# Seven products of a Strassen-like step, all in one matmul form, in 22 of 32 pairs

## The chip, the cores and the metric

The kernel runs on one core of one Trainium2 chip. The metric is the device time of one execution in microseconds (us); of three runs the median is 1759.95 us (1758.12 to 1761.29). Engines: PE (TensorE) multiplies matrices into PSUM, eight banks of 512 float32 columns on 128 partitions; DVE (VectorE) and ACT (ScalarE) do elementwise work and read PSUM; POOL (GpSimd) and SP (SyncE) here mostly issue DMAs. Each engine works its own instructions off in order and waits for semaphores.

## The reference

Two layers on 512 tokens of width 1024. Each layer has a feed-forward half step, a mixer (convolution, window attention and memory attention side by side) and a second feed-forward half step:

```python
def swiglu(x, w1, w3, w2):
    return (jax.nn.silu(x @ w1) * (x @ w3)) @ w2
...
        h = x + 0.5 * swiglu(rms_norm(x, ffn1_norm[l]), ffn1_w1[l], ffn1_w3[l], ffn1_w2[l])
        ...
        h = h + 0.5 * swiglu(rms_norm(h, ffn2_norm[l]), ffn2_w1[l], ffn2_w3[l], ffn2_w2[l])
```

`w1` and `w3` are 1024 x 2816 and `w2` is 2816 x 1024, all float32. So there are four feed-forwards, here called the parts, and they hold most of the matmul work.

## The kernel before

**Precision.** A float32 operand is split into two parts of a shorter format (`hi` by an ACT copy that rounds, `lo` by a DVE subtraction of `hi` from the operand). A product of two operands is three matmul passes: hi x hi, hi x lo, lo x hi. `split` (L147 to L149) does this, and `unit` (L357) does it for one weight tile of 128 x 1024 into a pair of tiles `whi` and `wlo`, of which there are four pairs in turn.

**The up projection.** The 2816 columns of `w1` and `w3` are 22 blocks of 128. The first four blocks of a part are computed plainly. The others go in pairs of blocks (f, f+1), nine in a part, through `up_pair` (L362). There each of the two matrices is multiplied by a two-by-two block scheme with seven products instead of eight: the weights of a pair and the activations (1024 rows in two halves, 512 tokens in two halves of 256) are added and subtracted in a fixed pattern, and seven products of 512 rows x 128 columns x 256 tokens are combined by additions. `Seven` (L297) prepares the seven moving operands `m[1]` to `m[7]`, each as four row blocks k, and each block with its hi part and its lo part of 256 columns beside each other. The weights' sums are made by DMAs that accumulate (the tile `wsum`, called X: block f by SP, then block f+1 added by POOL, L369 and L370) and, for the raw sums, by two DVE adds (L400) in the raw tile itself. A pair has seven weight units: raw and raw (one for each matrix; products 1 and 2), raw sum and raw sum (products 6 and 3), X and X (products 7 and 5), and z for both matrices (product 4).

**Two forms of a product.** `product` (L377) makes twelve matmuls of 256 columns that accumulate in one place: for each k, whi with the hi part and whi with the lo part, then four times wlo with the hi part. `beside` (L384) makes eight: four of 512 columns, in which whi meets the hi and the lo part at once and the two results stand beside each other in one PSUM bank, and four of 256 columns, wlo with the hi part, onto the first half. Whoever reads such a bank has to add its two halves, which takes one DVE add more. Before the change, products 1, 6 and 5 of each matrix are in the first form and 2, 3, 7 and 4 in the second; the first pair of each part (f = 4, `PLAIN`) has all of them in the first form, in a branch of its own. So 32 pairs are in the mixed form.

**Sums in PSUM.** Products 1, 6 and 5 of matrix i accumulate onto each other in the tile `x[i]` (tag "pt", two banks). After product 1 ACT copies it to `part[i]` (L438); after product 6 it copies the sum of both (L449), and after product 5 the sum of all three (L458). Products 2, 3, 7 and 4 have banks "po", "cf" and "mm", and `summed` (L402) adds both halves of such a bank and a part. Then come the SiLU (L467), the gate multiplication (L468), and the split of the gated result (L471, L472) for the down projection.

**Order.** The 22 blocks are worked off in quarters of 6, 6, 6 and 4 (`QUARTERS`). In each but the last, the up projection runs one pair ahead; then follows the down projection of the quarter, eight output blocks d with one weight unit each (L149 again, 768 columns) and one addition to the residual `h` (L564). So the pairs come in runs: f = 4 and 6 in the first quarter, 8, 10 and 12 in the second, 14, 16 and 18 in the third, 20 in the last. In the first feed-forward of a layer, the mixer's tables and memory keys (`prepare`) are computed after the first quarter's down projection, beside the second run of pairs.

The order on each engine is not the program's order: a scheduler that simulates the engines' time fills each engine's queue with what it expects to be ready. `tc.issue_after(x)` tells it that what follows is not to be issued ahead of x. Tiles come from pools with a fixed number of buffers, and a new tile waits until the old one in its buffer has been read: three for `raw` (raw, raw and z of a pair), three for X (tag "aux"), four for whi and wlo, one for `u`, two for `g`, two for `part`.

Of the kernel before, what the change touches and what calls it, by code (L numbers as in the profile page):

```python
# [13 lines left out]
AF = mybir.ActivationFunctionType  # L14
# [4 lines left out]
P = 128  # L19
# [8 lines left out]
QUARTERS = ((0, 6), (6, 6), (12, 6), (18, 4))  # L28
# [37 lines left out]
def trunk(ctx: ExitStack, tc: tile.TileContext, xT, memT, pos, w1a, w3a, w2a, w1b, w3b, w2b,  # L66
# [45 lines left out]
    first = []  # L112
# [243 lines left out]

    def unit(x):  # L357
        p = pair()
        split(p[0], p[1], x, V)
        return p  # L360

    def up_pair(l, w13, f, M):  # L362

        raw = [raw_tile(w13[i][l, f], D) for i in range(2)]
        X = []
        for i in range(2):

            x = wst.tile([P, UNIT], F32, tag="aux", name="wsum", bufs=3)
            nc.sync.dma_start(x.rearrange("p (f c) -> p f c", f=2), w13[i][l, f : f + 2, :, 0:QW].rearrange("f p c -> p f c"))  # L369
            G.dma_start(x, w13[i][l, f + 1], accum_op=ALU.add)  # L370
            X.append(x)
        z = wst.tile([P, UNIT], F32, tag="raw", name="raw", bufs=3)
        for i in range(2):
            nc.sync.dma_start(z[:, blk(i, QW)], w13[i][l, f + 1, :, QW:])
        x0, x1 = blk(0, QT), blk(1, QT)

        def product(ps, w, half, j, first=False):  # L377


            for n, (part, q) in enumerate([(0, q) for k in range(4) for q in ((k, 0), (k, 1))] + [(1, (k, 0)) for k in range(4)]):  # L380
                tail[0] = T.matmul(ps, w[part][:, blk(4 * half + q[0])], M.m[j][q[0]][:, q[1]], skip_group_check=True,  # L381
                                   start=first and not n, stop=n == 11)

        def beside(ps, w, half, j, first=False):  # L384


            def go(out, part, n):
                for k in range(4):
                    tail[0] = T.matmul(out, w[part][:, blk(4 * half + k)], M.m[j][k][:, 0:n], skip_group_check=True,  # L389
                                       start=first and not part and k == 0, stop=part == 1 and k == 3)  # L390

            go(ps, 0, 2)
            go(ps[:, 0], 1, 1)

        u, g = (tmp.tile([P, 2, S], F32, tag=t, name=t, bufs=n) for t, n in (("u", 1), ("g", 2)))
        part = [tm("part", "sq", 2) for _ in range(2)]
        to = (u, g)

        def add(out, a, b):
            V.tensor_tensor(out=out, in0=a, in1=b, op=ALU.add)  # L400

        def summed(out, ps, a):  # L402
            add(out, ps[:, 0], a)
            add(out, out, ps[:, 1])

        if f == PLAIN:
            xy = [bank([P, S], "po") for _ in range(2)]
            zv = [bank([P, S], "pt") for _ in range(2)]
            for i in range(2):
                w = unit(raw[i])  # L410
                product(xy[i][:, x0], w, 0, 1, first=True)
                product(xy[i][:, x1], w, 1, 2)
                A.activation(part[i], xy[i], AF.Copy)
                add(to[i][:, 0, x0], part[i][:, x0], part[i][:, x1])

                add(raw[i][:, 0:QW], raw[i][:, 0:QW], X[i][:, QW:])
                add(raw[i][:, QW:], raw[i][:, QW:], raw[i][:, 0:QW])
            for i in range(2):
                w = unit(raw[i])
                product(xy[i][:, x0], w, 0, 6)  # L420
                A.activation(part[i][:, x1], xy[i][:, x0], AF.Copy)
                product(zv[i][:, x0], w, 1, 3, first=True)
            for i in range(2):
                w = unit(X[i])
                product(xy[i][:, x0], w, 1, 5)
                A.activation(part[i][:, x0], xy[i][:, x0], AF.Copy)
                product(zv[i][:, x1], w, 0, 7)
                add(to[i][:, :, x1], zv[i].rearrange("p (n t) -> p n t", n=2), part[i][:, x0].unsqueeze(1).to_broadcast([P, 2, QT]))
            w = unit(z)
            for i in range(2):  # L430
                product(zv[i][:, x1], w, i, 4)
                add(to[i][:, 1, x0], zv[i][:, x1], part[i][:, x1])
        else:
            x = [bank([P, QT], "pt") for _ in range(2)]
            for i in range(2):
                w = unit(raw[i])
                product(x[i], w, 0, 1, first=True)
                A.activation(part[i][:, x0], x[i], AF.Copy)  # L438
                y = bank([P, 2, QT], "po")
                beside(y, w, 1, 2, first=True)  # L440
                summed(to[i][:, 0, x0], y, part[i][:, x0])

                add(raw[i][:, 0:QW], raw[i][:, 0:QW], X[i][:, QW:])
                add(raw[i][:, QW:], raw[i][:, QW:], raw[i][:, 0:QW])
            c, v = [bank([P, 2, QT], t) for t in ("cf", "mm")], []
            for i in range(2):
                w = unit(raw[i])
                product(x[i], w, 0, 6)
                A.activation(part[i][:, x1], x[i], AF.Copy)  # L449
                beside(c[i], w, 1, 3, first=True)  # L450
            for i in range(2):
                w = unit(X[i])
                v.append(bank([P, 2, QT], "po"))
                beside(v[i], w, 0, 7, first=True)
                A.activation(to[i][:, 1, x1], v[i][:, 0], AF.Copy)
                add(to[i][:, 1, x1], to[i][:, 1, x1], v[i][:, 1])
                product(x[i], w, 1, 5)
                A.activation(part[i][:, x0], x[i], AF.Copy)  # L458
                summed(to[i][:, 0, x1], c[i], part[i][:, x0])
                add(to[i][:, 1, x1], to[i][:, 1, x1], part[i][:, x0])  # L460
            w = unit(z)
            for i in range(2):
                beside(v[i], w, i, 4)
                summed(to[i][:, 1, x0], v[i], part[i][:, x1])
        out = gated()
        for n, sign in enumerate((1.0, -1.0)):
            A.activation(u[:, n], u[:, n], AF.Silu, scale=sign)  # L467
        M.gated = V.tensor_tensor(out=g, in0=g, in1=u, op=ALU.mult)  # L468
        for n, sign in enumerate((1.0, -1.0)):
            hi, lo = out[n]  # L470
            A.activation(hi, g[:, n], AF.Copy, scale=sign)  # L471
            V.scalar_tensor_tensor(out=lo, in0=g[:, n], scalar=sign, in1=hi.bitcast(F32), op0=ALU.mult, op1=ALU.subtract)  # L472
        return out

    def ffn(l, w13, w2, x, sums, factors, last, at_product, aside=None, closing=None):
# [60 lines left out]
        for q, (f0, nf) in enumerate(QUARTERS):  # L536
            ahead = 2 if q + 1 < len(QUARTERS) else 0
            for f in range(f0, f0 + nf + ahead, 2):
                if f not in g:
                    g[f], g[f + 1] = up_pair(l, w13, f, M)  # L540
                    if f == PLAIN:
                        with tc.issue_after(M.gated.ins):
                            rescale = after()
            begun = []

            def begin(d):

                w = weights(w2[l, d, :, f0 * P : (f0 + nf) * P], nf * P, V)
                ps = bank([P, S], "mm")
                for j in range(nf - 2):  # L550
                    mm3(ps, at(w, ALL, blk(j)), g[f0 + j], j == 0, False)
                begun.append((ps, w))

            for d in range(KD if ahead or not closing else KD - 2):
                while len(begun) < (d + 1 if ahead or d else 3):
                    with nullcontext() if ahead or d else queued():
                        begin(len(begun))
                ps, w = begun[d]
                for j in range(nf - 2, nf):
                    mm3(ps, at(w, ALL, blk(j)), g[f0 + j], False, j == nf - 1)  # L560
                if not q and rescale:
                    with tc.issue_after((added if d else M.gated).ins):
                        rescale(d)
                added = V.scalar_tensor_tensor(out=h[:, d, :], in0=ps, scalar=0.5, in1=h[:, d, :], op0=ALU.mult, op1=ALU.add)  # L564
                if not ahead:
                    last(d)
            if closing and not ahead:
                closing(l, f0, nf, g, [at(p, ALL, slice(0, nf * P)) for p in
                                       (weights(w2[l, d, :, f0 * P : (f0 + nf) * P], nf * P, V) for d in range(KD - 2, KD))])
            if aside and not q:  # L570
                aside(added)
# [751 lines left out]
```

## Time and profile before

| What | Value |
|---|---|
| median of three runs | 1759.95 us (1758.12 to 1761.29) |
| profiled execution, its own time | 1760.35 us |
| its span, first to last instruction | 1758.5 us |
| instructions | 26405, of them 10004 matmuls |
| busy share PE, PEld, DVE, ACT, POOL | 99%, 87%, 78%, 52%, 11% |
| granted PE clock, mean | 0.998 of full speed |
| HBM read | 249.67 MB, 143 GB/s over the span |

How to read it: the span runs from the first to the last instruction of one profiled execution; that execution's own time is 1.85 us more. A busy share counts the time in which an engine has at least one instruction in flight. PE's matmuls overlap, so that their lengths do not add up to time. PEld is the loading of weights ahead of a matmul, which overlaps with it. A group's row has the source line, the engine, the operation, what it writes and reads, the shape and the count; behind the bar stand the busy us, the mean ns of one, and the engine's idle time ahead of them with what ended it. A row of the timeline has the start and the length in us from the span's start; a bracket names the idle time ahead and what ended it.

### The profile page before, as it was taken

The numbers are of one execution on the slowest core, as the hardware profiler recorded it, in microseconds if no ns is written. First come the engines' busy times: TensorE is split into PE (matmuls) and PEld (weight loads), VectorE is DVE, ScalarE is ACT, GpSimd is POOL, SyncE is SP. The second block draws the span as 40 slices with busy tenths as digits, with TensorE's granted clock in tenths as the row PEclk, the third lists the DMA queues.
The fourth block names the chain that finished last, engine by engine and source line by source line (L and its number), as shares of the span: only waits on it lengthen the run. The fifth ranks groups of instructions, "written<-read, shape, count | busy, mean of one in ns | idle before, by whom it ended". The sixth has DMA issues, their size and how long they took to land.

```text
span 1758.5 us, 26405 instructions
## 1 busy us (share of the span) xinstructions
PE 1742.3 (99%) x10004; PEld 1524.0 (87%) x10004; DVE 1370.0 (78%) x2218; ACT 907.7 (52%) x1437; POOL 196.0 (11%) x220
## 2 busy tenths in 40 slices
PE   9999999999999999999999999999999999999997
PEld 7889889888888989898889898988888889898986
DVE  7969878689877868686778787776898768686866
ACT  6546445356765535353656354544567655453533
POOL 1001000006121000000010010000251210000000
PEclk9999999999999999999999999999999999999999
DMA  9456646257247546565566465542671666464632
GB/s 286 112 167 169 179 121 161 73 159 164 86 93 183 142 134 163 143 161 146 150 149 162 150 168 156 158 142 71 162 165 54 136 152 181 131 168 133 153 99 84
DMA packets 96335, 253.49 MB, mean 144 GB/s; under 512 B 9808, under 2 KB 16208, under 8 KB 96208
## 3 DMA queue, kind: packets, MB, share of 16 engines
q1 hardware_dynamic: 77200, 190.45, 34.8%
q0 software_dynamic: 19008, 61.35, 19.5%
q8 instruction: 79, 1.29, 0.3%
q14 instruction: 48, 0.39, 0.1%
HBM read 249.67 MB, written 2.10 MB: 143 GB/s over the span
## 4 chain that ended last, share of the span: by engine, by line
PE 92%; DVE 4%; DMA 2%; issue 1%; ACT 0%; SPq 0%; DVEq 0%; POOLq 0%; ACTq 0%
PE pt L381 16%; PE mm L180 14%; PE mm L182 14%; PE mm L181 14%; PE po L389 13%; PE po L381 2%; PE mm L389 2%; PE cf L389 2%; PE po L180 2%; PE po L182 2%; PE po L181 2%; PE po L928 2%; DMA wsum<-in_w3a 1%; PE mm L876 1%; PE cf L182 1%
## 5 line engine op out<-in xcount | busy, mean ns | idle before, releaser
L148 ACT ACTIVATE whi<-raw 128x1024 fp32r<-128x1024 f32 (+3 forms) x346 | 326.3, 947 | 429.1 <-PE mm L181 202.7
L149 DVE TENSOR_TENSOR wlo<-raw,whi 128x1024 fp32r<-128x1024 f32 (+3 forms) x346 | 374.7, 1088 | 99.4 <-ACT whi L148 98.2
L181 PE MATMUL mm<-glo,whi 128*128 128x512 f32 (+1 forms) x752 | 292.2, 389 | 0.0
L180 PE MATMUL mm<-ghi,whi 128*128 128x512 f32 (+1 forms) x752 | 292.0, 390 | 0.0
L182 PE MATMUL mm<-ghi,wlo 128*128 128x512 f32 (+1 forms) x734 | 285.3, 389 | 0.0
L564 DVE SCALAR_TENSOR_TENSOR h<-mm,h 128x512 f32<-128x512 f32 x126 | 86.3, 688 | 112.2 <-PE mm L182 111.8
L180 PEld LDWEIGHTS mm<-ghi,whi 128*128 128x128 f32 x752 | 141.2, 188 | 29.2 <-DVE h L564 1.2
L181 PEld LDWEIGHTS mm<-glo,whi 128*128 128x128 f32 x752 | 141.3, 188 | 28.4 <-DVE glo L472 0.2
L182 PEld LDWEIGHTS mm<-ghi,wlo 128*128 128x128 f32 x734 | 137.9, 188 | 27.7
L389 PE MATMUL po<-xlo,whi 128*128 128x512 f32 x512 | 139.5, 394 | 0.9 <-DVE g L400 0.9
L1058 DVE SCALAR_TENSOR_TENSOR there<-ypad,par,there 128x512 f32<-128x512 f32 x180 | 136.0, 779 | 1.3
L389 PEld LDWEIGHTS po<-xlo,whi 128*128 128x128 f32 x512 | 89.6, 189 | 15.2 <-DVE g L400 1.8
L180 PE MATMUL mm<-xhi,whi 128*128 128x512 f32 x256 | 101.6, 398 | 0.0
L182 PE MATMUL mm<-xhi,wlo 128*128 128x512 f32 x256 | 99.9, 390 | 0.0
L181 PE MATMUL mm<-xlo,whi 128*128 128x512 f32 x256 | 99.6, 389 | 0.0
L149 DVE TENSOR_TENSOR wlo<-wsum,whi 128x1024 fp32r<-128x1024 f32 x72 | 87.5, 1215 | 0.3 <-ACT whi L148 0.3
L389 PEld LDWEIGHTS po<-xlo,wlo 128*128 128x128 f32 x512 | 78.3, 188 | 10.6
L148 ACT ACTIVATE whi<-wsum 128x1024 fp32r<-128x1024 f32 x72 | 76.2, 1058 | 19.2 <-PE po L389 15.9
L381 PE MATMUL pt<-xhi,whi 128*128 128x256 f32 x576 | 81.9, 283 | 0.0
L389 PE MATMUL po<-xlo,wlo 128*128 128x256 f32 x512 | 81.2, 280 | 0.0
L381 PEld LDWEIGHTS pt<-xhi,whi 128*128 128x128 f32 x576 | 74.8, 190 | 0.5
L381 PE MATMUL pt<-ml,whi 128*128 128x256 f32 x512 | 72.9, 282 | 0.0
(397 smaller groups left out, 3605.7 us busy)
## 6 DMA issues: line engine op xcount, KB each, us to landing
raw<-in_w2a SPq DMA_DIRECT2D x48, 384.0 KB, 3.8
raw<-in_w2b SPq DMA_DIRECT2D x48, 384.0 KB, 3.7
raw<-in_w1a SPq DMA_DIRECT2D x26, 512.0 KB, 3.5
raw<-in_w3a SPq DMA_DIRECT2D x26, 512.0 KB, 3.7
raw<-in_w1b SPq DMA_DIRECT2D x26, 512.0 KB, 3.5
raw<-in_w3b SPq DMA_DIRECT2D x26, 512.0 KB, 3.6
wsum<-in_w1a SPq DMA_DIRECT2D x18, 512.0 KB, 4.5
wsum<-in_w3a SPq DMA_DIRECT2D x18, 512.0 KB, 3.6
```

The costliest lines, as they stand in the source:

```text
L148: a = A.activation(hi, x, AF.Copy)
L149: return a, on.tensor_tensor(out=lo, in0=x, in1=hi.bitcast(F32), op=ALU.subtract)
L180: T.matmul(ps, a[0], b[0], start=first, stop=False, **more)
L181: T.matmul(ps, a[0], b[1], start=False, stop=False, **more)
L182: tail[0] = T.matmul(ps, a[1], b[0], start=False, stop=last, **more)
L381: tail[0] = T.matmul(ps, w[part][:, blk(4 * half + q[0])], M.m[j][q[0]][:, q[1]], skip_group_check=True, start=first and not n, stop=n == 11)
L389: tail[0] = T.matmul(out, w[part][:, blk(4 * half + k)], M.m[j][k][:, 0:n], skip_group_check=True, start=first and not part and k == 0, st ...
L564: added = V.scalar_tensor_tensor(out=h[:, d, :], in0=ps, scalar=0.5, in1=h[:, d, :], op0=ALU.mult, op1=ALU.add)
L876: tail[0] = T.matmul(pp[i][:, z, :], q, k, start=not masked, stop=True, skip_group_check=True)
L928: tail[0] = T.matmul(po[:, 2 * c + i, :], ptb[:, i, j, :], v, start=(j == 0), stop=(j == nk - 1))
L1058: V.scalar_tensor_tensor(out=cv[:, c, :], in0=ypad[:, c, j : j + S], scalar=conv_w[:, c, j : j + 1], in1=cv[:, c, :], op0=ALU.mult, op1=AL ...
```

## The change

In 22 of the 32 mixed pairs, products 1, 6 and 5 also take the form of `beside`. These are the pairs with f > 12 in the first feed-forward of a layer (14, 16, 18, 20) and those with f > 6 in the second (8 to 20). The others run as before. For the 22:

- `x[i]` is a tile of two halves of 256 columns. After each of products 1, 6 and 5, ACT copies the first half to `part[i]`, and DVE adds the second half to it: six adds of 256 columns more in a pair.
- The units go matrix by matrix from the third on: raw sum, X of the first matrix, then raw sum, X of the second, then z. Before, both raw sums came ahead of both X.
- The two DVE adds that make a raw sum follow the DVE half of the split that came last ahead of them in the program (`unit.at`): for the first matrix that of the second raw tile, for the second matrix that of the first X. Before, they stood behind products 1 and 2 of their own matrix, without such an order.

```diff
     def unit(x):
         p = pair()
-        split(p[0], p[1], x, V)
+        unit.at = split(p[0], p[1], x, V)[1]
         return p
 
-    def up_pair(l, w13, f, M):
+    def up_pair(l, w13, f, M, full):
...
+        elif full:
+            x = [bank([P, 2, QT], "pt") for _ in range(2)]
+
+            def both(i, w, half, j, t, first=False):
+                beside(x[i], w, half, j, first)
+                A.activation(part[i][:, t], x[i][:, 0], AF.Copy)
+                add(part[i][:, t], part[i][:, t], x[i][:, 1])
+
+            for i in range(2):
+                w = unit(raw[i])
+                both(i, w, 0, 1, x0, True)
+                y = bank([P, 2, QT], "po")
+                beside(y, w, 1, 2, first=True)
+                summed(to[i][:, 0, x0], y, part[i][:, x0])
+            c, v = [bank([P, 2, QT], t) for t in ("cf", "mm")], []
+            for i in range(2):
+                with tc.issue_after(unit.at.ins):
+                    add(raw[i][:, 0:QW], raw[i][:, 0:QW], X[i][:, QW:])
+                add(raw[i][:, QW:], raw[i][:, QW:], raw[i][:, 0:QW])
+                w = unit(raw[i])
+                both(i, w, 0, 6, x1)
+                beside(c[i], w, 1, 3, first=True)
+                w = unit(X[i])
+                v.append(bank([P, 2, QT], "po"))
+                beside(v[i], w, 0, 7, first=True)
+                A.activation(to[i][:, 1, x1], v[i][:, 0], AF.Copy)
+                add(to[i][:, 1, x1], to[i][:, 1, x1], v[i][:, 1])
+                both(i, w, 1, 5, x0)
+                summed(to[i][:, 0, x1], c[i], part[i][:, x0])
+                add(to[i][:, 1, x1], to[i][:, 1, x1], part[i][:, x0])
+            w = unit(z)
+            for i in range(2):
+                beside(v[i], w, i, 4)
+                summed(to[i][:, 1, x0], v[i], part[i][:, x1])
         else:
...
-                    g[f], g[f + 1] = up_pair(l, w13, f, M)
+                    g[f], g[f + 1] = up_pair(l, w13, f, M, f > QUARTERS[2 if aside else 1][0])
```

## The prediction

> **What bounds the kernel now.** I read the page first, then the groups of TensorE instructions by shape, then the timeline of one run of pairs, then the windows by stage.
>
> ```profile
> span 1758.5 us, 26405 instructions
> ...
> PE 1742.3 (99%) x10004; PEld 1524.0 (87%) x10004; DVE 1370.0 (78%) x2218; ACT 907.7 (52%) x1437; POOL 196.0 (11%) x220
> ...
> PE 92%; DVE 4%; DMA 2%; issue 1%; ACT 0%; SPq 0%; DVEq 0%; POOLq 0%; ACTq 0%
> ```
>
> PE (TensorE) is busy for 99% of the span and carries 92% of the chain that ended last. So a change is worth what it takes from PE's pace, unless it makes PE wait. The next view must be read with care. Columns: count | busy us, mean ns of one | idle.
>
> ```profile
> L389 PE MATMUL po<-xlo,whi 128*128 128x512 f32 x512 | 139.5, 394 | 0.9 <-DVE g L400 0.9
> L381 PE MATMUL pt<-xhi,whi 128*128 128x256 f32 x576 | 81.9, 283 | 0.0
> ```
>
> The mean is how long one matmul is in flight, and matmuls overlap: in the first row 512 of them at 394 ns would be 201.7 us, yet their busy time is 139.5 us. What one costs is the distance from its start to the next start, and the timeline gives that. Columns: start, length, engine, line, operation, shape, count.
>
> ```profile
> 1528.33 1.11 PE L381 MATMUL pt<-ml,whi 128*128 128x256 f32 x8
> 1529.28 0.64 PE L381 MATMUL pt<-ml,wlo 128*128 128x256 f32 x4
> 1529.76 1.09 PE L389 MATMUL mm<-xhi,whi 128*128 128x512 f32 x4
> 1530.69 0.63 PE L389 MATMUL mm<-xhi,wlo 128*128 128x256 f32 x4
> 1531.16 1.09 PE L389 MATMUL po<-xlo,whi 128*128 128x512 f32 x4
> ...
> 1532.57 1.12 PE L381 MATMUL pt<-xhi,whi 128*128 128x256 f32 x8
> ```
>
> A product in twelve 256-column matmuls (L381) runs from 1528.33 to 1529.76, 1.43 us: 0.119 us each. A product in four of 512 and four of 256 columns (L389) runs from 1529.76 to 1531.16, 1.40 us, and the next to 1532.57, 1.41 us: 0.93/4 = 0.233 us for 512 columns, 0.47/4 = 0.118 for 256. A matmul of 512 columns costs nearly two of 256. So **one product gains 0.03 us, not the 0.7 us of the lengths** (12 x 0.283 - 4 x 0.394 - 4 x 0.283).
>
> Now the stages. Columns of the windows: from:to, length, then PE, PEld (weight loads), DVE, ACT, POOL busy with counts, PE clock, DMA share and GB/s.
>
> ```profile
> 142.30:203.50 61.20, 60.52 (x403) 55.25 (x403) 56.06 (x121) 35.73 (x63) 8.90 (x8) 1.00 0.70 178
> 1007.50:1069.00 61.50, 60.60 (x410) 55.50 (x409) 54.67 (x91) 37.93 (x63) 7.67 (x8) 1.00 0.62 169
> 1519.80:1579.00 59.20, 59.20 (x404) 54.87 (x403) 47.79 (x77) 32.02 (x51) 5.19 (x6) 1.00 0.66 168
> 1533.20:1557.30 24.10, 24.10 (x168) 22.45 (x167) 22.22 (x38) 14.02 (x24) 1.73 (x2) 1.00 0.64 170
> 1579.00:1612.00 33.00, 33.00 (x151) 27.42 (x150) 21.41 (x29) 10.74 (x14) 0.00 (x0) 1.00 0.46 129
> 1704.20:1724.10 19.90, 19.90 (x138) 18.45 (x138) 12.61 (x22) 9.78 (x17) 0.00 (x0) 1.00 0.25 67
> ```
>
> The 22 changed pairs stand in six stretches of three (the third row is one) and four of one (the last row); a down projection such as the fifth row follows each stretch of three. In the third row PE has no gap, and DVE (VectorE) is busy 47.79 of 59.20 us. **DVE is the engine to watch**: the change hands it work there. The first two rows are stretches of three pairs that are not changed, in which DVE also prepares the mixer's tables. There DVE is 92% and 89% busy, and PE needs 61.20 and 61.50 us for nearly the same matmuls (403 and 410 against 404), about 2.0 us more than without that load (2.3 less up to 6 matmuls for the second).
>
> **The change, part by part.**
>
> (1) *Products 1, 6 and 5 take the 512-column form.* Six products in a pair, 22 pairs: 132 x 0.03 = 4.0 us less on PE (with the 1.41 instead of the 1.40, 2.6 us), and 132 x 4 = 528 fewer matmuls and weight loads. All of it lies on the chain.
>
> (2) *132 more adds on DVE*, since the second operand part now stands in its own half of the bank and must be added after ACT's copy.
>
> ```profile
> 1514.00 0.69 DVE L400 TENSOR_TENSOR raw<-raw,wsum 128x512 f32<-128x512 f32 x1
> 1514.72 0.69 DVE L400 TENSOR_TENSOR raw<-raw 128x512 f32<-128x512 f32 x1
> ...
> 1531.98 1.23 DVE L149 TENSOR_TENSOR wlo<-raw,whi 128x1024 fp32r<-128x1024 f32 x1 [1.61 <-ACT whi L148]
> ...
> 1539.05 0.42 DVE L400 TENSOR_TENSOR g<-mm,part 128x256 f32<-128x256 f32 x1
> 1539.39 0.41 DVE L400 TENSOR_TENSOR g<-g,part 128x256 f32<-128x256 f32 x1
> ```
>
> An add of 256 columns is 0.41 us long and 0.34 from start to start: 18 in a stretch of three are 6.1 to 7.4 us. (3) *The raw sums of the second matrix* (1514.00 and 1514.72, 1.4 us, done ahead of a stretch that begins at 1519.8) now wait for the split of the first matrix's column sum, so they fall inside. DVE's load is then 47.8 + 6.1 to 7.4 + 1.4 = 55.3 to 56.6 us, and the stretch on PE 59.2 - 18 x 0.03 = 58.7 us: 94 to 96%. That leaves 2.1 to 3.4 us idle. The fourth row of the windows shows DVE in its densest part, 22.22 of 24.10 us, where it queues in order and still sits idle 8%, and PE there loses nothing. At 8%, 58.7 us want 4.7 us idle: DVE is short by 1.3 to 2.6 us in a stretch. Against that stands a lead: the split at 1531.98 ends at 1533.21 and is first used when the next pair starts, at 1538.24, 5 us later. So by sums the stretch can run out of slack and not of lead. In a single pair DVE goes from 12.61 to about 15 of 19.7 us, and in a down projection it has 33.00 - 21.41 = 11.6 us to catch up: both are costed at nothing, and if that cover were gone each would cost its DVE excess.
>
> (4) *A new wait.* Product 5 writes the bank in which product 6 was summed, so PE must now wait for DVE's add and not for ACT's copy alone; behind it on PE stands everything, in order.
>
> ```profile
> 1529.96 0.39 ACT L449 ACTIVATE part<-pt 128x256 f32<-128x256 f32 x1 [0.84 <-PE pt L381]
> ```
>
> The copy starts 0.2 us after the product's last matmul gave way to the next (1529.76). Product 6's chain is 0.2 + 0.39 + an operation of DVE's in hand (0 to 1.23) + 0.41 = 1.0 to 2.2 us. The two products between 6 and 5 last 2.8 us. It fits, unless two splits stand ahead of the add: then it is 0.6 us late. Bounds: never (0), or twice in each of 22 pairs (26 us). The nearest row is the dense part that cost PE nothing, so I take few: once in every second stretch of three, 3 x 0.6 = 1.8 us.
>
> (5) *Units go matrix by matrix, and with them the DMAs.* The first matrix's column sum is split one unit (two products, 2.8 us) earlier, the second matrix's raw sum one unit later.
>
> ```profile
> 1543.52 0.33 SPq L105 DMA_DIRECT2D raw<-in_w3b  x1
> 1548.95 0.38 SPq L369 DMA_DIRECT2D wsum<-in_w3b  x1
> ...
> 1553.01 0.86 POOL L370 DMA_DIRECT2D wsum<-in_w3b  x1 [20.34 <-DVE wlo L149]
> ...
> 1560.84 0.69 DVE L400 TENSOR_TENSOR raw<-raw,wsum 128x512 f32<-128x512 f32 x1 [3.06 <-DMA wsum<-in_w3b]
> ```
>
> The column sum of the second matrix is loaded (SP, 1548.95), accumulated (POOL, 1553.01), and DVE stands 3.06 us for it. It is now wanted two products later, so this wait shrinks to about 0.3 us. As DVE's idle time was counted above, it is no further supply, but an in-order stall is gone from the tightest place. Against it, the next pair's second raw load (1543.52) waits for a split that comes 2.8 us later, and SP's next loads queue behind it.
>
> ```profile
> raw<-in_w3b SPq DMA_DIRECT2D x26, 512.0 KB, 3.6
> ...
> L148 ACT ACTIVATE whi<-raw 128x1024 fp32r<-128x1024 f32 x206 | 217.9, 1060 | 264.7 <-PE mm L181 153.3 <-PE pt L381 27.9 <-PE po L389 23.8
> ```
>
> The split comes by product 8 of one pair, and the load is wanted at product 2 of the next, 8 products or 11 us later. Landing (3.6 us), ACT's copy (1.06) and DVE's split (1.23) take 5.9: covered; if not, the pair is late by the difference. No count of DMAs changes. (6) *The wider PSUM tiles* take the same number of banks. *The last pair's tail* has one add more before its gating: at most 4 x 0.34 = 1.4 us, taken as 0, since that add belongs to product 5 and is followed by two products of 1.4 us.
>
> [...]
>
> **The sum**: -4.0 (1) + 1.8 (4) = -2.2 us. The profiled execution took 1760.35 us (span 1758.5 and 1.85 around it), which gives 1758.1; the median of the runs is 0.4 below the profiled one, so **1757.8 us**.
>
> **The rivals.**
>
> *B, the cover holds everywhere*: PE never waits, -4.0 us, 1756.0. For it: the dense 24.10 us without a gap, the 5 us of lead, the vanished 3.06 us wait. Against: 94 to 96% is above the dense part's 92%.
>
> *C, DVE becomes the pace in the stretches of three*, the other side. For it stand the first two rows of the windows, and in the second of them PE's own waits:
>
> ```profile
> 1052.75 1.21 PE L389 MATMUL po<-xlo,whi 128*128 128x512 f32 x4 [0.37 <-DVE g L400]
> ...
> 1055.70 0.70 PE L389 MATMUL po<-mh,whi 128*128 128x512 f32 x2 [0.48 <-DVE u L400]
> ```
>
> PE stands twice for a bank that DVE has not yet read. At 2.0 us a stretch, six cost 12, and the sum is -4.0 + 12 = +8.0: 1768.0. It decides once the idle 2.1 to 3.4 us are less than the queue needs and the lead is spent. Against it: those two stretches carry table work in long blocks, which the changed ones do not.
>
> *D, weight loads set the pace.* Eight loads for twelve would make a product 1.43 x 8/12 = 0.95 us, and the gain 132 x 0.48 = 63 us: 1697. The rows speak against it: the eight-load form takes 1.40 us. [...]
>
> *E, the lengths are the cost*: 132 x 0.7 = 92 us, 1668; the 1.40 against 1.43 us excludes it but for a misreading.
>
> That the change does less than it says I leave out: pairs 14 to 20 of two feed-forwards and 8 to 20 of the other two are 2 x 4 + 2 x 7 = 22.
>
> **How the numbers follow.** Forecast 0.42, B 0.28, C 0.28, D and E 0.01 each. 0.2% is 3.5 us, about what a measurement of this kernel can tell from no change. The forecast, with 0.6 to 7.5 us given back (1756.5 to 1763.4), lies within it; B lies just beyond, C on the other side. Faster: 0.28 + 0.02 = 0.30; the same 0.42; slower 0.28. The range runs from B less 1.5 us (the scatter of the runs shown, 1758.12 to 1761.29, about their median) to C: 1754.5 to 1768.5.
>
> **What will show it.** Step 1: L381 falls by 132 x 12 matmuls, L389 gains 528 of each shape, a product still takes 1.40 us, and a stretch of three 58.7 us. Steps 2 and 3: DVE 55 to 57 us busy in a stretch. Step 4: PE rows that wait for a DVE add into `part` ahead of product 5, 1 or 2 in all, or many if C holds. Step 5: no DVE wait of 3 us for wsum. I am wrong if PE's gaps in the six stretches sum to more than 7.5 us, or if products of 512 columns run faster than 1.40 us.

## The result, and the profile after

The kernel after takes **1777.18 us** (median; 1775.07 to 1778.6). Against 1759.95 us this is 17.2 us more: a ratio of 1.010 with a 95% interval of 1.0088 to 1.0112. The forecast of 1757.8 us and its range up to 1768.5 are both missed on the slow side. The profiled execution has a span of 1775.9 us, 17.4 more than before, so the trace holds the whole loss.

First the page of the kernel after: the span, the engines, the shares of the chain that ended last, and two groups.

```profile
span 1775.9 us, 25484 instructions
...
PE 1745.9 (98%) x9476; PEld 1499.7 (84%) x9476; DVE 1403.8 (79%) x2350; ACT 904.3 (51%) x1437; POOL 196.3 (11%) x220
...
PE 79%; DVE 13%; issue 4%; DMA 3%; ACT 1%; SPq 0%; DVEq 0%; POOLq 0%; ACTq 0%
...
L389 PE MATMUL po<-xlo,whi 128*128 128x512 f32 x512 | 140.9, 397 | 13.7 <-DVE g L400 11.3
...
L400 DVE TENSOR_TENSOR part<-part,pt 128x256 f32<-128x256 f32 x132 | 54.0, 412 | 18.3 <-ACT part L438 18.3
```

528 matmuls are gone as planned, and the 132 new adds are there (last row). DVE's part of the chain rose from 4% to 13%, and PE's fell from 92% to 79%. One group holds most of it: PE stood 13.7 us ahead of the first matmuls into a bank `po`, where it stood 0.9 us before, and it stood for DVE. Yet DVE's share of the span is 79%, one point more than before; nothing in the busy shares shows the cause.

The time by stages, taken between the same matmuls in both traces, from the first of a run of three pairs to the first after the down projection behind it: 92.13 to 92.98 us before, and 95.86, 95.56, 93.95, 93.81, 97.11 and 93.81 us after. The six sum to 16.3 us more. The four single pairs are shorter, 19.54 us instead of 19.82, and what comes behind each takes 0.3 to 0.7 us longer, 1.9 us in all. The first run of three starts 0.3 us later. 16.3 - 1.1 + 1.9 + 0.3 = 17.4 us is the difference of the spans.

Windows by stage of the kernel before, then of the kernel after (the columns are those of the prediction's windows): one run of three with its down projection, and its three pairs alone.

```profile
650.70:742.84 92.14, 92.14 (x554) 82.29 (x553) 69.20 (x106) 42.83 (x65) 5.18 (x6) 1.00 0.57 154
650.70:707.34 56.64, 56.64 (x394) 52.81 (x393) 47.19 (x76) 32.09 (x51) 4.45 (x6) 1.00 0.64 168
```

```profile
655.07:750.63 95.56, 93.72 (x481) 79.92 (x480) 73.96 (x124) 42.48 (x65) 5.17 (x6) 0.98 0.55 149
655.07:715.12 60.05, 58.21 (x321) 50.44 (x320) 52.54 (x92) 31.62 (x51) 5.17 (x6) 0.97 0.63 169
```

All of the loss lies in the three pairs (60.05 against 56.64 us), none in the down projection. Over the stage DVE has 4.8 us more work, in 124 instead of 106 instructions; in the three pairs it is busy for 52.54 of 60.05 us, so that 7.5 us of idle time are left. DVE was not full over the stretch, and PE stood for it all the same. The timeline tells where. PE of the kernel after, at the end of two runs of three:

```profile
1579.50 0.63 PE L389 MATMUL pt<-ml,wlo 128*128 128x256 f32 x4
1582.23 1.76 PE L389 MATMUL po<-xlo,whi 128*128 128x512 f32 x4 [2.10 <-DVE g L400]
1583.79 1.05 PE L389 MATMUL po<-xlo,wlo 128*128 128x256 f32 x4
```

```profile
702.79 0.52 PE L389 MATMUL pt<-ml,wlo 128*128 128x256 f32 x3
705.12 1.85 PE L389 MATMUL po<-xlo,whi 128*128 128x512 f32 x4 [1.81 <-DVE g L400]
```

PE wants a bank `po` that DVE has not yet read out. DVE in front of the first of these waits:

```profile
1568.48 1.22 DVE L149 TENSOR_TENSOR wlo<-raw,whi 128x1024 fp32r<-128x1024 f32 x1 [1.61 <-ACT whi L148]
...
1577.41 0.68 DVE L400 TENSOR_TENSOR raw<-raw,wsum 128x512 f32<-128x512 f32 x1
1578.01 0.74 DVE L400 TENSOR_TENSOR part<-part,pt 128x256 f32<-128x256 f32 x2
1578.67 1.21 DVE L502 TENSOR_TENSOR g<-g,u 128x1024 f32<-128x1024 f32 x1
1579.81 0.68 DVE L400 TENSOR_TENSOR raw<-raw 128x512 f32<-128x512 f32 x1
1580.41 0.41 DVE L400 TENSOR_TENSOR g<-po,part 128x256 f32<-128x256 f32 x1
1580.75 0.41 DVE L400 TENSOR_TENSOR u<-po,part 128x256 f32<-128x256 f32 x1
1581.08 0.68 DVE L506 SCALAR_TENSOR_TENSOR glo<-g,ghi 128x512 fp32r<-128x512 f32 x1
1581.68 0.41 DVE L400 TENSOR_TENSOR g<-g,po 128x256 f32<-128x256 f32 x1
```

The add at 1581.68 reads the bank; it ends at 1582.09, and PE goes on at 1582.23. Ahead of it DVE stands in no row: from 1568.48 on, one operation begins as the last one gives way. A window over this run of the kernel after, and over the run that answers to it in the kernel before:

```profile
1568.48:1587.09 18.61, 15.48 (x77) 13.07 (x76) 18.61 (x34) 9.24 (x16) 1.72 (x2) 0.91 0.56 126
```

```profile
1560.84:1577.65 16.81, 16.81 (x113) 15.37 (x112) 16.77 (x29) 9.22 (x16) 1.73 (x2) 1.00 0.60 147
```

**This is the row I had not read.** In the kernel before, DVE already works without a gap for the last 16.8 us of the run of three, and PE does not stand. The timelines of the six runs that were to be changed show it in each: DVE works without a gap for 9.1 us about the border of the first and the second pair, for 7.6 us in the second, and for 16.8 us in the third (gaps of up to 0.07 us not counted). In the third pair there was no idle time to take an add from. After, the first two rows have grown into one of 20.2 us and the third to 18.6 us in the run shown, and all three into a single one of 38.8 us in the run from 655.07.

### The profile page after: what moved, and what is told of

Its sections match the earlier page's. It is cut to its first block, busy times and chain, and to the rows that moved or that the text cites. A ratio compares the mean times of both kernels' runs of the same rounds, so it can differ in the third digit from the quotient of the medians.

```text
span 1775.9 us, 25484 instructions
## 1 busy us (share of the span) xinstructions
PE 1745.9 (98%) x9476; PEld 1499.7 (84%) x9476; DVE 1403.8 (79%) x2350; ACT 904.3 (51%) x1437; POOL 196.3 (11%) x220
## 4 chain that ended last, share of the span: by engine, by line
PE 79%; DVE 13%; issue 4%; DMA 3%; ACT 1%; SPq 0%; DVEq 0%; POOLq 0%; ACTq 0%
PE mm L180 14%; PE mm L181 13%; PE mm L182 13%; PE po L389 8%; PE pt L389 5%; PE pt L381 5%; DVE wlo L149 3%; DVE g L400 2%; PE po L381 2%; DVE raw L400 2%; DVE u L400 2%; PE mm L389 2%; PE po L180 2%; PE po L181 2%; PE po L182 2%
## 5 line engine op out<-in xcount | busy, mean ns | idle before, releaser
L148 ACT ACTIVATE whi<-raw 128x1024 fp32r<-128x1024 f32 (+3 forms) x346 | 325.8, 946 | 432.9 <-PE mm L181 187.1
L389 PE MATMUL po<-xlo,whi 128*128 128x512 f32 x512 | 140.9, 397 | 13.7 <-DVE g L400 11.3
L389 PEld LDWEIGHTS po<-xlo,whi 128*128 128x128 f32 x512 | 89.8, 190 | 29.0 <-issue 12.1
L148 ACT ACTIVATE whi<-wsum 128x1024 fp32r<-128x1024 f32 x72 | 76.1, 1057 | 36.0 <-PE mm L181 30.2
L389 PEld LDWEIGHTS po<-xlo,wlo 128*128 128x128 f32 x512 | 78.9, 191 | 9.4
L389 PE MATMUL po<-xlo,wlo 128*128 128x256 f32 x512 | 83.8, 283 | 0.0
L438 ACT ACTIVATE part<-pt 128x256 f32<-128x256 f32 x132 | 47.5, 373 | 58.1 <-PE pt L389 52.5
L400 DVE TENSOR_TENSOR part<-part,pt 128x256 f32<-128x256 f32 x132 | 54.0, 412 | 18.3 <-ACT part L438 18.3
L501 ACT ACTIVATE u<-u 128x512 f32<-128x512 f32 x72 | 44.1, 625 | 45.3 <-DVE u L400 45.1
```

The source lines that it names most:

```text
L148: a = A.activation(hi, x, AF.Copy)
L438: A.activation(part[i][:, t], x[i][:, 0], AF.Copy)
```

## The experiments

Four readings stood against each other. *Load*: the adds' DVE time makes DVE late along a run of three, and PE stands for whatever DVE is late with. *Order*: the new order of units makes PE stand, not the adds. *Bank*: the ring of banks `po` is the fault, and another bank would do. *Wait*: PE's new wait of product 5 for the add behind product 6 is itself the fault. Ratios are against the kernel before in the same comparison, with 95% intervals. The scheduler orders each of these kernels anew, so that besides its edit each also differs a little in the order of its instructions.

### The order alone

```diff
-            x = [bank([P, 2, QT], "pt") for _ in range(2)]
+            x = [bank([P, QT], "pt") for _ in range(2)]
-                beside(x[i], w, half, j, first)
-                A.activation(part[i][:, t], x[i][:, 0], AF.Copy)
-                add(part[i][:, t], part[i][:, t], x[i][:, 1])
+                product(x[i], w, half, j, first)
+                A.activation(part[i][:, t], x[i], AF.Copy)
```

> The changed kernel's unit order, matrix by matrix, and its place for the raw sums, but products 1, 6 and 5 in the twelve-matmul form, without the six adds. Theory load (the 132 added DVE adds fill the queue, and PE stands for a PSUM bank of tag po that DVE reads late): 1759 to 1762 us, no PE wait above 1 us in a stretch of three pairs. Theory order (product 7 now comes two products after product 3 of its own matrix, so the po bank that product 2 filled is wanted earlier): 1768 to 1775, with the same waits before a po product as in the changed kernel.

Measured: 1760.79 us against 1758.74, 1.0012 [1.0002, 1.0021]. The stage took 92.54 us (before 92.14) with 68.57 us of DVE, and its trace shows a wait of PE of 0.31 us in each of the six runs. The order by itself costs some 2 us and not 17.

### The form alone, in the old order

```diff
+                add(raw[i][:, 0:QW], raw[i][:, 0:QW], X[i][:, QW:])
+                add(raw[i][:, QW:], raw[i][:, QW:], raw[i][:, 0:QW])
             c, v = [bank([P, 2, QT], t) for t in ("cf", "mm")], []
             for i in range(2):
-                with tc.issue_after(unit.at.ins):
-                    add(raw[i][:, 0:QW], raw[i][:, 0:QW], X[i][:, QW:])
-                add(raw[i][:, QW:], raw[i][:, QW:], raw[i][:, 0:QW])
                 w = unit(raw[i])
                 both(i, w, 0, 6, x1)
                 beside(c[i], w, 1, 3, first=True)
+            for i in range(2):
                 w = unit(X[i])
```

> All seven products in the 512-column form with the six adds, but the units and raw sums in the order of the kernel before. Theory load: 1768 to 1780, PE waits of 1 to 2 us before po products late in a stretch of three. Theory order: 1754 to 1757, since the saving of 0.05 us a product (14 products of a single pair took 19.54 us in the changed kernel against 19.82) stays and the cause is gone.

Measured: 1786.85 us against 1758.74, 1.0163 [1.0148, 1.0178], above the ranges of both theories. In each run of three PE stands once for 2.6 to 3.9 us, not for a bank but for weights: ACT's half of the second matrix's raw sum, ahead of its product 3. In one of the runs (the timeline, DVE, ACT and PE):

```profile
695.90 0.69 DVE L400 TENSOR_TENSOR raw<-raw,wsum 128x512 f32<-128x512 f32 x1 [3.13 <-issue]
...
698.51 0.68 DVE L400 TENSOR_TENSOR raw<-raw 128x512 f32<-128x512 f32 x1
...
699.28 1.06 ACT L148 ACTIVATE whi<-raw 128x1024 fp32r<-128x1024 f32 x1 [0.21 <-DVE raw L400]
...
700.39 1.80 PE L389 MATMUL mm<-xhi,whi 128*128 128x512 f32 x4 [3.76 <-ACT whi L148]
```

DVE stands 3.13 us ahead of that sum (1.8 to 3.1 us in the six runs), at the place where it stood for the DMA of `wsum` before, and puts six other adds between the sum's two. So 28.1 us are lost with the form alone and 17.2 with form and order together: the new order saves about 10 us of what the form costs. Most of this is half clock (last section): this trace has seven lengths of 3.41 us of it in the runs of three and a mean granted clock of 0.992, that of the kernel after two and 0.997; at 1.6 us a length that is some 8 us of difference. The order is a part of the remedy, not of the fault, and PE's stand is not tied to `po`.

### The form and the order without the adds

```diff
                 A.activation(part[i][:, t], x[i][:, 0], AF.Copy)
-                add(part[i][:, t], part[i][:, t], x[i][:, 1])
```

> The changed kernel without its six adds in a pair: the second halves of products 1, 6 and 5 are left out of the sums. Same matmuls, same unit order. Theory load: 1753 to 1756, no PE wait above 1 us in the stretches. Theory order: 1768 to 1775, waits as in the changed kernel.

Measured: 1755.97 us against 1758.74, 0.9985 [0.9975, 0.9995]. The stage takes 91.50 us, and PE has no gap in it:

```profile
651.80:743.30 91.50, 91.50 (x481) 78.50 (x480) 68.89 (x106) 42.69 (x65) 5.19 (x6) 1.00 0.57 155
```

With the adds goes the whole loss, in spite of the same form and order. But two things leave together: the time of the adds, and PE's wait for them. The next runs part these.

### The load alone, on the kernel before

An operation of DVE's is put behind each ACT copy in the same 22 pairs. It takes the larger of `part` and `part`, which changes nothing; the form, the written order and PE's waits stay those of before.

```diff
+        def extra(i, t):
+            if full:
+                V.tensor_tensor(out=part[i][:, t], in0=part[i][:, t], in1=part[i][:, t], op=ALU.max)
...
                 A.activation(part[i][:, x0], x[i], AF.Copy)
+                extra(i, x0)
```

> The kernel before, and after each of ACT's copies into part a DVE instruction of 256 columns over the same place (the maximum of part with itself, which changes nothing), in the same 22 pairs: the changed kernel's DVE load without its matmul form, its order and its new wait of PE. Theory load: 1766 to 1778. Theory that the new wait of product 5 for the DVE add is what costs: 1759 to 1762. Theory order: 1759 to 1762.

Measured: 1773.74 us against 1758.74, 1.0091 [1.0076, 1.0106]. The page's group of the new operations, the window of the stage, and the stand of PE in it:

```profile
L408 DVE TENSOR_TENSOR part<-part 128x256 f32<-128x256 f32 x132 | 54.8, 419 | 0.0
```

```profile
652.20:747.50 95.30, 92.71 (x553) 82.19 (x552) 75.11 (x124) 43.14 (x65) 5.19 (x6) 1.00 0.57 149
```

```profile
695.90 1.20 PE L389 MATMUL po<-xlo,whi 128*128 128x512 f32 x4 [2.44 <-DVE g L400]
```

132 operations of the adds' length, with nothing else in the program changed, cost 15.0 us, with a stand of 1.5 to 2.6 us at the bank `po` in each run. They read no PSUM, so it is DVE's time that costs, without the form, the order and the new wait. As a sum it does not close: the change gave back 21.9 us (17.2 and the 4.7 that its form gains, below), and this run has the old order of units.

### Adds of the same count, but short

```diff
-                add(part[i][:, t], part[i][:, t], x[i][:, 1])
+                add(part[i][:, t][:, 0:16], part[i][:, t][:, 0:16], x[i][:, 1, 0:16])
```

> The changed kernel with its six adds in a pair over 16 of 256 columns; the other columns of the second halves of products 1, 6 and 5 are left out of the sums. The adds keep their places, their waits for ACT's copy and PE's wait for them, but take less of DVE's time. Theory DVE time: most of the loss goes, 1756 to 1764. Theory in-order waits (DVE stands for ACT's copy ahead of each add, and PE for the add): it stays, 1770 to 1778.

Measured: 1753.89 us against 1759.2, 0.9968 [0.9957, 0.9979].

```profile
L400 DVE TENSOR_TENSOR part<-part,pt 128x16 f32<-128x16 f32 x132 | 20.8, 165 | 9.8 <-ACT part L438 9.8
```

```profile
650.02:741.56 91.54, 91.54 (x481) 78.54 (x480) 70.17 (x124) 42.80 (x65) 5.17 (x6) 1.00 0.57 156
```

All 132 adds and all of PE's dependencies on them are there; an add lasts 0.165 us instead of 0.41. PE has no gap in the stage, and the time is 5.3 us under that of before, below even the range of the theory that it bears out. So neither the count of the adds, nor PE's wait as such, nor DVE's own wait for ACT's copy ahead of them (9.8 us in the row above) costs anything, and *wait* falls as a cause of its own: the adds' time does it. (The scheduler has put 24 instead of 16 matmuls of the third pair behind the first of the down projection here.) The 91.54 us also give the gain of the form with DVE out of the way: 92.14 - 91.54 = 0.60 us for 18 products, 0.033 us each, with the new order in it.

### Another bank for product 2

```diff
-                y = bank([P, 2, QT], "po")
+                y = bank([P, 2, QT], "mm")
```

> The changed kernel with product 2's result in a bank of tag mm (three banks) instead of po (two), so that product 7 does not wait for product 2's bank to be read. Theory DVE load: the wait moves to another bank or split, since DVE is late whatever it is late with: 1772 to 1782. Theory bank ring (two po banks are the bottleneck and DVE's lateness would be harmless with more): 1756 to 1765, and no PE wait above 1 us before a po product.

Measured: 1778.81 us against 1759.2, 1.0117 [1.0102, 1.0132]. The long stand at `po` is gone (0.3 us of idle time at most are left). In its place PE stands 2.3 us in each run of three ahead of product 6 of the second matrix, which writes `pt`; the trace puts this to ACT's half of a weight split (`whi`, L148), so it is no bank that is wanted there. The time stays. *Bank* falls.

### Which pairs of a run

Four kernels have the change in some pairs only; the rest run as before. The edit is the condition in the call, here for the first pairs (with the single ones); the others have, for the third pairs, `(18,)` and `(12, 18)`; for the first without the single pairs, `(14,)` and `(8, 14)`; for the first and second, `(14, 16)` and `(8, 10, 14, 16)`.

```diff
-  up_pair(l, w13, f, M, f > QUARTERS[2 if aside else 1][0])
+  up_pair(l, w13, f, M, f in ((14, 20) if aside else (8, 14, 20)))
```

> The changed form only in the first pair of each stretch of three and in the single pairs, 10 pairs instead of 22. Theory that the load adds up along a stretch until the lead is spent: DVE's idle time in the first pair takes the adds, and the saving 10 x 6 x 0.05 = 3 us remains: 1755 to 1758. Theory that each changed pair costs by itself (in-order waits of DVE for ACT's copies in every pair): 17 x 10/22 = 8 us more than before, 1764 to 1769.

> The changed form only in the first pair of each stretch of three, 6 pairs, the single pairs as before. Where all 10 pairs had it, the single pairs took 0.28 us less each, but the mixer or the end behind them began 0.4 to 0.8 us later. Theory that a late gate in the last pair gives that back: the 6 pairs keep 6 x 0.28 = 1.7 us and lose nothing, 1756.5 to 1758, faster than the 10 pairs by about 1 us. Rival, that the difference behind the single pairs is the scheduler's and not theirs: no better than the 10 pairs, 1758 to 1760.

> The changed form in the first and second pair of each stretch of three, 12 pairs; the third pair and the single pairs as before. Theory that DVE's load adds up along a stretch: the second pair's adds fall where DVE was already 92% busy, so PE stands at a bank late in the stretch, 1 to 2 us in each of six: 1763 to 1770. Rival, that only the third pair is tight, because the down projection's weight splits follow it: 12 x 0.28 = 3.4 us saved, 1755 to 1757.

> The changed form only in the third pair of each stretch, 6 pairs. Theory that the load adds up along a stretch: DVE is already dense there but has its lead, so 6 x 2.3 us of adds come on top of little slack: 1758 to 1763. Theory that each changed pair costs by itself: 17 x 6/22 = 5 us more, 1762 to 1766.

| Changed pairs | Adds in each run of three | Time, and before in the same comparison | Ratio |
|---|---|---|---|
| first of each run, and the four single | 6 | 1758.37, 1759.2 us | 0.9996 [0.9986, 1.0005] |
| first of each run | 6 | 1757.75, 1758.46 us | 0.9995 [0.9986, 1.0004] |
| first and second | 12 | 1765.4, 1758.46 us | 1.0035 [1.0023, 1.0047] |
| third of each run | 6 | 1772.42, 1759.2 us | 1.0076 [1.0061, 1.0091] |
| all 22 | 18 | 1777.18, 1759.95 us | 1.010 [1.0088, 1.0112] |

The same six adds cost nothing measurable in the first pair and 13.2 us in the third. Both theories for the third pairs had missed: 1772.42 us lies above 1763 and 1766. The first pairs with the single ones came 0.4 us above the range of their theory, and the gain of about 1 us from leaving the single pairs out did not show. The first and second pairs came as the first theory had it. Windows of the stage with the change in the first pairs (the kernel that has it in the single pairs too), then in the third:

```profile
650.14:742.07 91.93, 91.93 (x529) 81.09 (x528) 70.71 (x112) 42.62 (x65) 5.18 (x6) 1.00 0.57 155
```

```profile
651.70:745.79 94.09, 92.48 (x530) 81.01 (x528) 71.26 (x112) 43.45 (x65) 5.18 (x6) 1.00 0.54 151
```

DVE has nearly the same work in both stages, 70.71 and 71.26 us, and one loses 2 us where the other gains 0.2. So a sum of DVE's work over the stage does not decide; the place does. DVE in the third pair works without a gap before the change, and six adds of 0.34 us are 2.0 us. Measured: 13.2/6 = 2.2 us a run. (One stretch at half clock, 1.6 us, is in the 13.2, and the gain of 36 products, 1.2 us, has been taken off; without both it is 2.1 us a run.) The size is that of the adds, but that each pushes all behind it by its pitch is not shown: in this kernel DVE's row is broken, as it stands 0.93 us for PE at 694.32. In the first pair there are gaps to take the adds: in the run from 650 DVE has 4.8 us of idle time ahead of its row of 9.1 us, and with the change in the first pairs alone 3.2 us are left there and the row is 11.6 us. With twelve adds the first two rows have grown into one of 20.1 us in the run looked at, and 6.9/6 = 1.2 us of the adds' 12 x 0.34 = 4.1 come through.

With the change in the third pairs alone, the stand shows as the prediction's step 4 had drawn it (the timeline, ACT, DVE and PE):

```profile
698.53 0.38 ACT L438 ACTIVATE part<-pt 128x256 f32<-128x256 f32 x1 [0.82 <-PE pt L389]
698.85 1.28 DVE L506 SCALAR_TENSOR_TENSOR glo<-g,ghi 128x512 fp32r<-128x512 f32 x2
700.05 0.68 DVE L400 TENSOR_TENSOR raw<-raw 128x512 f32<-128x512 f32 x1
700.65 0.41 DVE L400 TENSOR_TENSOR part<-part,pt 128x256 f32<-128x256 f32 x1
701.12 1.20 PE L389 MATMUL pt<-xhi,whi 128*128 128x512 f32 x4 [1.22 <-DVE part L400]
```

ACT's copy ends at 698.91, and the add behind it starts 1.74 us later, since three operations of DVE's stand ahead of it. Product 5 waits 1.2 to 1.4 us here in all six runs, and some 8 us later the first matmuls of the down projection wait another 0.3 to 1.8 us for ACT's half of a weight split. So the new wait can be where a part of the loss appears. The short adds show that it is not what the loss is made of: the queue on DVE is.

No kernel of these that computes everything is faster than before by more than the measurement can tell.

## Why the prediction was wrong

**What bounds the kernel** was read rightly: PE's pace, with DVE the engine to watch. The size of the change was not.

**Step 1, the gain of the form: right.** L381 fell from 2976 matmuls to 1392, by the 1584 foreseen, and L389 gained 528 of each shape. A product in the new form:

```profile
1572.97 1.09 PE L389 MATMUL pt<-mh,whi 128*128 128x512 f32 x4
1573.90 0.63 PE L389 MATMUL pt<-mh,wlo 128*128 128x256 f32 x4
1574.37 1.09 PE L389 MATMUL cf<-xhi,whi 128*128 128x512 f32 x4
```

It takes 1574.37 - 1572.97 = 1.40 us, as foreseen, with 0.93/4 = 0.233 us for 512 columns. The gain is 0.033 us a product in the runs of three (from the stage with the short adds) and 0.28/6 = 0.047 in the single pairs: 108 x 0.033 + 24 x 0.047 = 4.7 us against 4.0. Rivals D and E are excluded.

**Step 2, the adds' own price: right.** 0.412 us long (page after), 0.34 from start to start.

**Step 3 failed, in the sentence "Against that stands a lead".** Its sum had DVE short of idle time by 1.3 to 2.6 us a run of three, and measured is a loss of 1.0 to 5.0 us a run, 2.7 in the mean (16.3/6). The step then costed this shortage at nothing, because a split ended 5 us before its use. That was one split, the first of the row of 9.1 us, with 1.61 us of idle time ahead of it, and a split of weights, while what PE ran out of in the kernel after was a bank. The lead at the bank stood in the same trace of before. Here are, in the third pair, the adds that free the two banks `po`, and the matmuls of product 7 that take them next (the timeline, DVE and PE):

```profile
1570.51 0.41 DVE L400 TENSOR_TENSOR u<-u,po 128x256 f32<-128x256 f32 x1
...
1572.11 1.09 PE L389 MATMUL po<-xlo,whi 128*128 128x512 f32 x4
...
1573.51 0.41 DVE L400 TENSOR_TENSOR g<-g,po 128x256 f32<-128x256 f32 x1
...
1575.06 1.09 PE L389 MATMUL po<-xlo,whi 128*128 128x512 f32 x4
```

The adds end at 1570.92 and 1573.92, 1.2 and 1.1 us ahead. In the first pair of this run the lead is 7.4 us, in the second 3.2 to 3.3; the other five runs have the same, and 1.1 to 1.8 us in the third. So the lead was nearly spent by the end of a run before the change took any of it. And the window of 1560.84 to 1577.65 shows 16.77 of 16.81 us. Step 3 took the stretch from 1533.20 to 1557.30, at 92%, as "its densest part" and as proof that a dense stretch costs nothing. The densest part lay behind it, and the row at 1560.84 stood in the prediction, quoted for its DMA wait; what follows it was not read.

**Step 4 failed in its size.** From bounds of 0 and 26 us it took 1.8 us, by the dense part "that cost PE nothing". Given back were 17.2 + 4.7 = 21.9 us, by the gain of step 1. PE's long stands at the bank `po` in the six runs sum to 14.7 us (1.5, 2.27, 1.97, 1.9, 1.79, 1.19, 2.26 and 1.77); two stretches at half clock cost another 3.2 (below); the places behind the single pairs 1.9. The remaining 2.1 us, some 0.3 in each run, are not assigned to a cause. The step also named one wait, that of product 5, and the stand was elsewhere in the kernel after: PE stands for whatever DVE comes to last, a bank here, weights in some of the other kernels.

**Step 5, the 3.06 us wait for wsum: right, and its worth not seen.** In the run from 655.07 to 715.12 DVE no longer waits for `wsum`; it waits 3.3 us, in five pieces, for ACT's half of splits instead. The idle time had been counted with the supply, so the step gave it no price. The form alone shows one: with the adds in the old order, DVE stands in that place, and PE stands 2.6 to 3.9 us in each run for the sum behind it. With the new order the same adds cost about 10 us less, most of it half clock.

**Step 6, the tail: wrong.** It was bounded at 1.4 us and taken as 0; behind the single pairs 1.9 us were measured (0.3 to 0.7 four times). The cover named, two products of 1.4 us behind the last such add, did not hold it. The traces of the two kernels with the change in the first pairs agree: behind the four single pairs 2.8 us more than before where these have the change, 0.4 where they do not; as times the two cannot be told apart (0.9996 and 0.9995). The page after shows a part: 1.0 us of PE's idle time ahead of the down projection's first matmuls, for ACT's half of the gated result:

```profile
L180 PE MATMUL mm<-ghi,whi 128*128 128x512 f32 (+1 forms) x752 | 292.4, 391 | 1.1 <-ACT ghi L505 1.0
```

**The rivals.** B fell. C had the mechanism: DVE sets the pace in the runs of three, and PE stands for banks that it has not read. Its price of 2.0 us a run came from pairs with table work; measured is 16.3/6 + 0.6 = 3.3 us a run, with the half clock in it, so the true time lies above C's 1768.0 and outside the range. Half of C's condition, "once the idle 2.1 to 3.4 us are less than the queue needs", was also put wrongly: 7.5 us of idle time were left in the run of 60.05 us and did not help, because they lay ahead of DVE's row of 38.8 us (4.8) and behind it (2.6). The other half, that the lead is spent, came true.

## What to carry to other kernels

Before giving an engine more work, do not divide its busy time by the stage: find its long rows of work without a gap, here the 16.8 us at the end of each run of three, where six adds cost 2.2 us, while the same adds in a place with gaps cost nothing. The length of the row alone is not the sign: the kernel with the short adds has one of 18.5 us (665.87 to 684.35) in the first two pairs of a run, and PE stands nowhere. What counts is how far the engine is ahead of those who wait for it. One comfortable lead proves nothing for the next pair; follow the lead along the run to its end, here from 7.4 to 3.2 to 1.2 us. The probe that settles such a case is cheap: put the extra operations into the kernel before without using them, and shorten them in the kernel after without removing them.

## What was not expected of the hardware

After two of its stands PE came back at half clock. Windows of the kernel after, right behind them:

```profile
705.10:708.50 3.40, 3.38 (x11) 2.81 (x12) 3.40 (x6) 2.36 (x4) 0.86 (x1) 0.53 0.41 63
1582.20:1585.60 3.40, 3.37 (x11) 2.87 (x12) 3.40 (x6) 2.37 (x4) 0.83 (x1) 0.55 0.54 81
```

The granted clock there is 0.53 and 0.55; it is 0.50 from 705.34 to 708.75 and from 1582.56 to 1585.97, 3.41 us each time. Each costs 1.6 us, 3.2 of the 17 us: the twelve matmuls from 705.12 to 709.06 take 3.94 us and those from 1582.23 to 1586.18 take 3.95, where the starts of step 1 give 0.93 + 0.47 + 0.93 = 2.33. The two stands, between the matmuls that ought to follow each other, were 1.97 and 2.26 us long. A stand of 2.27 us that ends at 287.11 in the same execution was followed by full clock (1.00 from 287 to 291), and so was one of 2.60 us with the load alone (mean clock 0.998 there, as in the kernel before). With the form alone there were five such stretches, two of them of 6.8 us (mean clock 0.992); with product 2 in another bank four (0.995), with the change in the third pairs one (0.997). So the stand of 1.97 us cost 3.6 us with its half clock, nearly twice its length. The length alone does not tell which stand does: 2.26 us was followed by half clock and 2.27 us was not. What decides between them is not shown.

A smaller one: the form gains 0.047 us a product in the single pairs and 0.033 in the runs of three, where the new order is in the number. Why these differ was not looked into.
